# The first mixer's work and loads put into two written-out orders, and the sweep's raw weight tiles given places of their own

## The chip, the core and the metric

The kernel runs on one core of a Trainium2 chip. The metric is the device time of one execution in microseconds (us). Three executions of the kernel before took 917.3, 917.93 and 917.94 us; the median is 917.93 us. A change of about 0.2% (1.8 us) is what a measurement of this kernel can tell from none.

## The reference, cut to what matters

A decoder of two layers on 512 tokens of width 1024, float32. Layer 0 mixes tokens by pooling, layer 1 by a gated spatial unit; each is followed by a squared-ReLU MLP of width 4096. Six vectors per layer (shift, scale and gain for the mixer and for the MLP) come from one conditioning vector `c`.

```
mod = silu(c) @ ada_w[i] + ada_b[i];  sh1, sc1, g1, sh2, sc2, g2 = split(mod, 6)
h = rmsnorm(x, norm_mix_g[i]) * (1 + sc1) + sh1
layer 0:  y = per group of 256 channels: (windowed mean over 2, 4, 8, 16 tokens - h) @ pool_w, * pool_scale
x = x + g1 * y
h = rmsnorm(x, norm_mlp_g[i]) * (1 + sc2) + sh2
x = x + g2 * (square(relu(h @ w1[i])) @ w2[i])
```

The change touches the first mixer and the start of the first MLP only.

## The kernel before, in words

The big products run in three passes of high and low parts (`mm3`, L123: lines 125, 126, 127 of the profile are those passes), so TensorE (PE) is what most of the span is made of. VectorE (DVE) and ScalarE (ACT) prepare operands; every large load is issued by SyncE (SP) through one queue, in the order in which SP's instructions stand.

**The mixer** works on four groups of 256 channels, `g` = 0 to 3. What it needs from memory, in tiles of 512 KB:

- `x`, four tiles; `m`, 16 columns of `ada_w` (four a group, name `m` + group + number), each multiplied with silu(c) and summed by one DVE instruction (`column`, L251 to L255);
- the gains: for groups 0 and 1 two tiles `ag` that PE multiplies (`gains`, L285), for groups 2 and 3 two columns `gt` each (`gain_cols`, L295) that PE spreads over the partitions (`gain_spread`, L305);
- `pw`, the pooling weights, 256 KB a group, scaled by the gain in `weigh` (L309).

Per group: `windows` (PE, L324) takes the windowed means of x, `fin` (DVE, L269 to L274) finishes scale and shift from the four columns, `pooled` (ACT, L330) applies them, `product` (PE, L338) multiplies with pw, `add` (DVE, L345) adds into x, `sums_of` (L214 on ACT, L216 on DVE) sums squares for the next norm, `turn` and `turned` (PE L357, ACT L361) transpose x into `xf`. When the sums of all four groups are there, POOL takes the root (`power`, L168), ACT and DVE build diagonals, and PE spreads the norms (`rb`, L470).

**The sweep** (L475 to L489) is the first part of the MLP's first product: for each of eight blocks `k` of 128 channels, seven banks each get three matmuls, 168 in all. Block k needs `ht` (DVE L478), `hh` (ACT L479), `hl` (DVE L482), the weight tile `raw` of 448 KB (`sweep_load`, L380) split into a high part (ACT L386) and a low part (DVE L389), and, for the block's scale and shift, two more columns of `ada_w` (`ada`, L368).

Places in SBUF: the pool `w4` has three tiles, the pools `wh` and `wl` five each. Columns and gain tiles of the mixer take these 13 places in turn (`get_any`, L246); the sweep's `raw` tiles take `w4` places too (L381), and its columns go on taking all 13 in turn. A load into a place waits until the tile's last reader is done.

The order of DVE's and ACT's instructions in the mixer and the sweep is that in which the code is written (L391 to L487, from `gains(0)` on: group by group, in the order 0, 1, 2, 3); PE's is too. SP's order is left to the scheduler, which starts from the order in which the loads are written beside their consumers.

Of the kernel before, what the change touches and what calls it, by code (L numbers as in the profile page):

```python
# [35 lines left out]
def c_sc(n, k):  # L36
    return 24 * n + 2 * k
# [6 lines left out]
def c_g(n, k):  # L44
    return 24 * n + 16 + k


@with_exitstack
def decoder_kernel(ctx: ExitStack, tc: tile.TileContext, xtok, vecs, rows, fgrow, ada0, adag, ada1, pool_w, w1s, w1, w2, w2e, w_v, w_u, w_o, wsT, lnp, bs, out):
# [46 lines left out]
    shift(sm, 88)  # L96
# [81 lines left out]
    with (  # L178
        tc.tile_pool(name="st", bufs=1) as st,
        tc.tile_pool(name="st2", bufs=2) as st2,  # L180
        tc.manual_schedule(engines={mybir.EngineType.DVE, mybir.EngineType.Activation}),
# [40 lines left out]
        V.tensor_copy(cab, ca.unsqueeze(2).to_broadcast([P, KD, P]))  # L222
# [20 lines left out]
        slots = [(w4, "w4")] * 3 + [(wts, "wh"), (wts, "wl")] * 5
        nslot = [0]

        def get_any():  # L246
            pool, tag = slots[nslot[0] % len(slots)]
            nslot[0] += 1
            return pool.tile([P, D], F32, name="ada", tag=tag) if pool is w4 else wtile(tag, F32)

        def column(src, out):  # L251

            r = get_any()
            nc.sync.dma_start(r, src)
            V.scalar_tensor_tensor(r, r, 1.0, cb, ALU.mult, ALU.mult, accum_out=out)  # L255
# [3 lines left out]
        def m(g, *js):

            if g not in pm4:
                pm4[g] = sm.tile([P, 4], F32, name="pm4", tag="pm4")
            for j in js:
                column(ada0[4 * g + j], pm4[g][:, j : j + 1])

        def fin(g):
            win = 2 << g
            c, k = slice(4 * g, 4 * g + 4), slice(2 * g, 2 * g + 2)
            V.tensor_tensor(mods[0][:, c], pm4[g], vec[:, V_ADAB + c.start : V_ADAB + c.stop], ALU.add)  # L269
# [4 lines left out]
            V.tensor_tensor(bg, bg, sh, ALU.subtract)  # L274
# [3 lines left out]
        pw = st.tile([P, KD, 256], F32, name="pw")  # L278
        pgs, dgs = {}, {}

        def load_pw(g):
            c = slice(2 * g, 2 * g + 2)
            nc.sync.dma_start(pw[:, c], pool_w[:, c])

        def gains(g):  # L285
            po = pgs[g] = bank("pg", xz)[:, 0:256]
            for j in range(2):
                r = get_any().rearrange("p (k c) -> p k c", k=4)
                nc.sync.dma_start(r, adag[g, j])
                for k in range(4):  # L290
                    T.matmul(po, cab[:, 4 * j + k], r[:, k], start=(j + k == 0), stop=False)  # L291
            T.matmul(po, ones[0:1, :], row[0:1, D + 256 * g : D + 256 * g + 256], start=False, stop=True)
# [87 lines left out]
        def sweep_load(k):  # L380
            r = w4.tile([P, D], F32, name="raw", tag="w4")  # L381
            nc.sync.dma_start(r[:, 0 : P * SWEEP], w1s[k])
# [8 lines left out]
        gains(0)  # L391
        windows(0)
        m(0, 0, 1)
        weigh(0)
        m(0, 2, 3)
        fin(0)
        pooled(0)
        windows(1)
        gains(1)
        m(1, 0, 1)  # L400
        product(0)
        weigh(1)
        m(1, 2)
        add(0, 0)
        add(0, 1)
        m(1, 3)
        fin(1)
        pooled(1)
        for t in range(NT):
            sums_of(0, t)  # L410
        windows(2)
        gain_cols(2)
        product(1)
        turn(0)
        turned(0)
        gain_spread(2)
        m(2, 0)
        add(1, 0)
        weigh(2)
        m(2, 1)  # L420
        add(1, 1)
        m(2, 2, 3)
        fin(2)
        pooled(2)
        for t in range(NT):
            sums_of(1, t)
        windows(3)
        turn(1)
        turned(1)
        gain_cols(3)  # L430
        product(2)
        gain_spread(3)
        m(3, 0)
        weigh(3)
        m(3, 1)
        add(2, 0)
        add(2, 1)
        m(3, 2, 3)
        fin(3)
        pooled(3)  # L440
        for t in range(NT):
            sums_of(2, t)
        turn(2)
        turned(2)
        s3 = sm.tile([P, NT], F32, name="s3", tag="rv4")
        V.tensor_reduce(s3, ssg[:, :, 0:3], mybir.AxisListType.X, ALU.add)
        V.tensor_scalar(s3, s3, RMS_EPS, None, ALU.add)
        ada(0, 0)
        ada(0, 1)
        sweep_load(0)  # L450
        product(3)
        add(3, 0)
        sums_of(3, 0)
        sums_of(3, 1, V)
        sweep_hi(0)
        add(3, 1)
        sums_of(3, 2)
        sums_of(3, 3, V)
        V.tensor_tensor(s3, s3, ssg[:, :, 3], ALU.add)
        r4 = power(s3, NT)  # L460
        sweep_lo(0)
        turn(3)
        diag = st.tile([P, NT, P], F32, name="diag")
        rb = bank("rb", xz)
        for t in range(NT):
            if t % 2:
                V.tensor_scalar(diag[:, t], ident, r4[:, t : t + 1], None, ALU.mult)
            else:
                A.activation(diag[:, t], ident, AF.Copy, scale=r4[:, t : t + 1])
            T.matmul(rb[:, tok[t]], ones, diag[:, t], start=True, stop=True)  # L470
        turned(3)
        ada(1, 0)


        sweep = [bank("po") for _ in range(4)] + [bank("po", xz) for _ in range(SWEEP - 4)]  # L475
        for k in range(KD):
            t = st2.tile([P, S], F32, name="ht", tag="ht")
            V.scalar_tensor_tensor(t, xf[:, k], scl[0][1][:, k : k + 1], rb, ALU.mult, ALU.mult)  # L478
            A.activation(hh[:, k], t, AF.Identity, bias=mod(0, c_sh(1, k)))  # L479
            if k and k + 1 < KD:  # L480
                ada(k + 1, 0)
            V.scalar_tensor_tensor(hl[:, k], t, mod(0, c_sh(1, k)), f32(hh[:, k]), ALU.add, ALU.subtract)  # L482
# [481 lines left out]
```

## Time and profile before

| what | value |
|---|---|
| median of three executions | 917.93 us |
| the profiled execution's own time | 919.2 us |
| its span in the trace | 917.1 us |
| PE busy, share of the span | 877.8 us, 96% |
| DVE busy | 653.8 us, 71% |
| ACT busy | 419.9 us, 46% |
| POOL busy | 54.3 us, 6% |
| read from memory | 135.87 MB |
| mean granted clock of TensorE | 0.984 |

The times below are those of the profiled execution, counted from the start of its span, so they are compared with 917.1 and not with the median. The first sweep matmul starts at 74.99 us, the last of the 168 at 129.09 us. PE counts as busy while a matmul is in flight, at whatever clock, so a busy share near 100% can still hide slow matmuls: one of 512 columns takes a step of 0.23 us at the full granted clock and 0.43 us at half.

### The profile page before, as it was taken

What the parts mean: (1) busy time and instruction counts of PE and PEld (TensorE: products, weight loads), DVE (VectorE), ACT (ScalarE), POOL (GpSimd) and SP (SyncE); (2) the same over time, 40 slices, a digit from 0 to 9 for tenths busy, and PEclk for the clock granted to TensorE, in tenths of its full rate; (3) what the DMA queues carried; (4) which work ended last, traced back from release to release, by engine and by line L of the source; (5) the groups of instructions that cost most, each with busy time, mean ns of one, the idle gap of its engine ahead of it and who ended that gap; (6) DMA issues with size and microseconds to landing.
All of it is one profiled execution on the core that took longest, in us unless ns stands there. A gap on an engine that the chain in (4) does not pass through costs nothing.

```text
span 917.1 us, 10446 instructions
## 1 busy us (share of the span) xinstructions
PE 877.8 (96%) x3980; PEld 723.3 (79%) x3980; DVE 653.8 (71%) x846; ACT 419.9 (46%) x609; POOL 54.3 (6%) x102
## 2 busy tenths in 40 slices
PE   8766899999999999999999999999999999999996
PEld 5655678878888888888878888988887888888885
DVE  4855679778886888955798845557677576667954
ACT  4343375544544445436532425645545444444521
POOL 6000000300000000000310000000004000000000
PEclk9977999999999999999999999999999999999999
DMA  9915676355355342442547412741433134112212
GB/s 339 410 51 179 226 245 228 138 184 195 132 194 198 132 163 90 150 172 92 184 178 243 139 38 98 267 163 46 160 138 125 36 116 171 58 48 91 92 46 91
DMA packets 35475, 138.64 MB, mean 151 GB/s; under 512 B 3937, under 2 KB 4065, under 8 KB 32225
## 3 DMA queue, kind: packets, MB, share of 16 engines
q1 hardware_dynamic: 35282, 137.72, 42.2%
q8 instruction: 31, 0.51, 0.2%
q10 hardware_dynamic: 144, 0.26, 0.1%
q14 instruction: 18, 0.15, 0.0%
HBM read 135.87 MB, written 2.10 MB: 150 GB/s over the span
## 4 chain that ended last, share of the span: by engine, by line
PE 87%; DVE 5%; DMA 3%; ACT 2%; issue 1%; SPq 0%; POOL 0%; POOLq 0%; DVEq 0%; ACTq 0%
PE po L126 16%; PE po L127 16%; PE po L125 16%; PE pm L126 11%; PE pm L127 11%; PE pm L125 11%; DMA wh<-in_ada 2%; PE po L338 1%; PE pg L291 1%; DMA ada<-in_adag 1%; PE po L813 1%; DVE wl L255 1%; PE pb L161 1%; DVE wh L255 1%; DVE wl L389 1%
## 5 line engine op out<-in xcount | busy, mean ns | idle before, releaser
L125 PE MATMUL po<-hh,wl 128*128 128x512 f32 (+1 forms) x608 | 233.9, 385 | 7.7 <-ACT hh L479 7.7
L126 PE MATMUL po<-hl,wh 128*128 128x512 f32 (+1 forms) x608 | 232.6, 383 | 3.8 <-DVE hl L482 2.5
L127 PE MATMUL po<-hh,wh 128*128 128x512 f32 (+1 forms) x608 | 231.6, 381 | 0.0
L117 DVE TENSOR_TENSOR wl<-b,wh 128x1024 fp32r<-128x1024 f32 x84 | 102.7, 1224 | 70.1 <-ACT wh L116 70.0
L117 DVE TENSOR_TENSOR wl<-raw,wh 128x1024 fp32r<-128x1024 f32 x89 | 108.7, 1223 | 47.7 <-ACT wh L116 47.3
L125 PEld LDWEIGHTS po<-hh,wl 128*128 128x128 f32 x608 | 115.5, 190 | 32.0 <-ACT hh L479 9.7
L126 PEld LDWEIGHTS po<-hl,wh 128*128 128x128 f32 x608 | 115.5, 190 | 28.6 <-DVE hl L482 5.0
L127 PEld LDWEIGHTS po<-hh,wh 128*128 128x128 f32 x608 | 115.4, 190 | 21.3
L127 PE MATMUL pm<-wh,oh 128*128 128x512 f32 x336 | 130.7, 389 | 0.0
L125 PE MATMUL pm<-wh,ol 128*128 128x512 f32 x336 | 130.7, 389 | 0.0
L126 PE MATMUL pm<-wl,oh 128*128 128x512 f32 x336 | 130.7, 389 | 0.0
L116 ACT ACTIVATE wh<-raw 128x1024 fp32r<-128x1024 f32 x89 | 94.2, 1058 | 52.5 <-PE pm L127 33.4
L517 ACT ACTIVATE g<-po 128x512 f32<-128x512 f32 x64 | 37.9, 598 | 167.1 <-PE po L127 167.1
L116 ACT ACTIVATE wh<-b 128x1024 fp32r<-128x1024 f32 x84 | 88.4, 1053 | 14.2 <-PE pm L127 9.6
L147 DVE SCALAR_TENSOR_TENSOR ada<-ada,cb 128x1024 f32<-128x1024 f32 x56 | 68.2, 1221 | 16.6 <-DMA ada<-in_ada 16.5
L125 PEld LDWEIGHTS pm<-wh,ol 128*128 128x128 f32 x336 | 63.1, 188 | 13.2
L126 PEld LDWEIGHTS pm<-wl,oh 128*128 128x128 f32 x336 | 63.1, 188 | 13.1
L127 PEld LDWEIGHTS pm<-wh,oh 128*128 128x128 f32 x336 | 63.1, 188 | 13.0
L699 ACT ACTIVATE tmp<-x 128x512 f32<-128x512 f32 (+1 forms) x25 | 15.3, 613 | 64.9 <-DVE x L695 64.9
L617 DVE TENSOR_TENSOR y<-y,pm 128x512 f32<-128x512 f32 x68 | 43.4, 680 | 0.0
L518 ACT ACTIVATE g<-g 128x512 f32<-128x512 f32 x64 | 39.6, 624 | 0.0
L158 POOL TENSOR_SCALAR dg<-ident,mods 128x128 f32<-128x128 f32 x24 | 25.6, 1083 | 227.6 <-DVE wl L117 129.2
(164 smaller groups left out, 1163.1 us busy)
## 6 DMA issues: line engine op xcount, KB each, us to landing
ada<-in_ada SPq DMA_DIRECT2D x64, 512.0 KB, 3.3
raw<-in_w SPq DMA_DIRECT2D x57, 512.0 KB, 3.3
b<-in_w SPq DMA_DIRECT2D x24, 1024.0 KB, 4.8
raw<-in_w2e SPq DMA_DIRECT2D x16, 512.0 KB, 3.3
wh<-in_ada SPq DMA_DIRECT2D x14, 512.0 KB, 9.5
wl<-in_ada SPq DMA_DIRECT2D x14, 512.0 KB, 9.5
ur<-in_w_u SPq DMA_DIRECT2D x8, 512.0 KB, 5.9
raw<-in_w_v SPq DMA_DIRECT2D x8, 512.0 KB, 4.6
```

What stands on the lines that cost most here:

```text
L116: A.activation(h, r, AF.Copy)
L117: V.tensor_tensor(l, r, f32(h), ALU.subtract)
L125: T.matmul(o, wl, mh, start=first, stop=False, **kw)
L126: T.matmul(o, wh, ml, start=False, stop=False, **kw)
L127: T.matmul(o, wh, mh, start=False, stop=last, **kw)
L147: V.scalar_tensor_tensor(r, r, 1.0, cb, ALU.mult, ALU.mult, accum_out=pmv[i, b][:, j : j + 1])
L158: G.tensor_scalar(dg[:, k], ident, cols[:, k : k + 1], None, ALU.mult)
L255: V.scalar_tensor_tensor(r, r, 1.0, cb, ALU.mult, ALU.mult, accum_out=out)
L517: A.activation(t, po, AF.Relu)
L518: A.activation(t, t, AF.Square)
L617: V.tensor_tensor(yt, yt, banks[hf], ALU.add)
L699: A.activation(tmp, xt, AF.Square, scale=D**-0.5, accum_out=s[:, len(cs) : len(cs) + 1])
```

## The change

1. The mixer and what follows it up to the sweep is no longer written as calls in a row. A string `WORK` lists each piece of work (`m03`: the column 3 of group 0; `win`, `pd`, `pr`, `ad`, `sm`, `tn`, `td`: windows, pooled, product, add, sums, turn, turned; `gm`, `gt`, `gc`, `bc`, `we`: gain product, gain column, its finish, its spread, weigh; `hi`, `lo`: the split of a raw tile), and a loop carries them out in that order. A string `LOADS` lists the loads in their own order; a load is emitted as soon as the reader that its place waits for has been emitted. The four groups are now interleaved, and groups 0, 2, 1, 3 reach their product in that order.
2. SP joins the engines whose order is kept as written.
3. The sweep's `raw` tiles have two places of their own (pool `st2`). The sweep's columns (`n`) take only the three `w4` places.
4. The partial columns of each group have their own small tiles; `fin` forms the window term in one DVE instruction instead of two. Padding of the small pool goes from 88 to 64 words, and the large tiles that stay keep their addresses.

After the sweep the order of the instructions differs only within the first few units of the MLP.

```diff
+LOADS = """
+    gt20 m01 m03 gt31 x m02 m00 ag0 m22 gt21 m33 m20 pw0 m23 m21 m13 pw2 m12 ag1 m10 pw1 m11 pw3 m31 m32
+    gt30 m30 n01 raw0 n00
+"""
+WORK = """
...
+    gt30 pd1 pr2 m30 ad20 pr1 hi0 ad10 gc3 tn0 m31 win3 td0 ad11 fin3 ad21 pd3 bc3 sm11 sm03 sm12 we3
+    tn1 sm10 lo0 pr3 ad30 sm21 sm20 sm23 sm22 sm00 sm13 s3 sm30 sm31V ad31 td1 tn3 sm32 sm33V tot tn2
...
+"""
-        tc.manual_schedule(engines={mybir.EngineType.DVE, mybir.EngineType.Activation}),
+        tc.manual_schedule(engines={mybir.EngineType.DVE, mybir.EngineType.Activation, mybir.EngineType.SP}),
...
+        def places(name):
+
+            kind = name.rstrip("0123456789")
+            if kind == "n":
+                return slots[0:1]
+            return [slots[(nslot[0] + j) % len(slots)] for j in range({"ag": 2, "m": 1, "gt": 1}.get(kind, 0))]
...
+            def free(pool, tag):
+                bufs = 3 if pool is w4 else 5
+                return len(taken[tag]) < bufs or taken[tag][-bufs]
+
+            while queue and all(free(*at) for at in places(queue[0])):
+                load(queue.pop(0))
...
-            V.tensor_scalar(bg, sh, float(win), 1.0 / win, ALU.mult, ALU.mult)
-            V.tensor_tensor(bg, bg, sh, ALU.subtract)
+            V.scalar_tensor_tensor(b0[:, k], sh, win * (1.0 / win), sh, ALU.mult, ALU.subtract)
...
         def sweep_load(k):
-            r = w4.tile([P, D], F32, name="raw", tag="w4")
+            r = st2.tile([P, D], F32, name="raw", tag="raw")
             nc.sync.dma_start(r[:, 0 : P * SWEEP], w1s[k])
-            wk[k] = r[:, 0 : P * SWEEP], *(t[:, 0 : P * SWEEP] for t in wpair())
+            wk[k] = [r[:, 0 : P * SWEEP]]
 
         def sweep_hi(k):
+            wk[k] += [t[:, 0 : P * SWEEP] for t in wpair()]
             A.activation(wk[k][1], wk[k][0], AF.Copy)
...
+        for op in WORK.split():
+            on_v, op = op.endswith("V"), op.rstrip("V")
...
+            loads()
...
         for k in range(KD):
-            A.activation(hh[:, k], t, AF.Identity, bias=mod(0, c_sh(1, k)))
-            if k and k + 1 < KD:
-                ada(k + 1, 0)
+            norm_hi(k)
             if k + 1 < KD:
-                sweep_load(k + 1)
+                queue += [f"n{k + 1}0", f"raw{k + 1}", f"n{k + 1}1"]
+                loads()
+                n_(k + 1, 0)
+                norm_lo(k)
                 sweep_hi(k + 1)
-                ada(k + 1, 1)
+                n_(k + 1, 1)
                 sweep_lo(k + 1)
```

On SP, from the mixer's last loads into the sweep, the order before was this (`raw` are the sweep's weight tiles; `ada`, `wh` and `wl` with source `in_ada0` are columns, named by the place that they take):

```order
L254 DMA wh_487<-in_ada0 128x1024
L254 DMA wl_490<-in_ada0 128x1024
L382 DMA raw_496<-in_w1s 128x896
L254 DMA ada_544<-in_ada0 128x1024
L382 DMA raw_558<-in_w1s 128x896
L254 DMA ada_563<-in_ada0 128x1024
L254 DMA ada_595<-in_ada0 128x1024
L382 DMA raw_599<-in_w1s 128x896
L382 DMA raw_640<-in_w1s 128x896
L382 DMA raw_681<-in_w1s 128x896
L254 DMA wh_604<-in_ada0 128x1024
L254 DMA wl_636<-in_ada0 128x1024
```

Now it is this, from the last columns of the mixer (`wh_284`: gt30, `wl_287`: m30) on:

```order
L280 DMA wh_284<-in_ada0 128x1024
L280 DMA wl_287<-in_ada0 128x1024
L280 DMA ada_326<-in_ada0 128x1024
L430 DMA raw_328<-in_w1s 128x896
L280 DMA ada_330<-in_ada0 128x1024
L280 DMA ada_551<-in_ada0 128x1024
L430 DMA raw_553<-in_w1s 128x896
L280 DMA ada_555<-in_ada0 128x1024
L280 DMA ada_592<-in_ada0 128x1024
L430 DMA raw_594<-in_w1s 128x896
L280 DMA ada_596<-in_ada0 128x1024
```

Each block now loads one column, its raw tile and its other column, in the order in which they are used; before, three raw tiles stood ahead of a block's second column.

On DVE, up to the end of `fin(3)`, the place before (`wh_442` to `wl_456` are the columns m30 to m33; `po` are products of group 2; `mods0`, `scl00`, `b0` are fin's):

```order
L255 SCALAR_TENSOR_TENSOR wh_442,pm4_441<-wh_442,cb_89 128x1024
L312 TENSOR_TENSOR gp_445<-pg_439,psb_175 128x256
L314 TENSOR_TENSOR pw_202<-pw_202,gp_445 128x512
L255 SCALAR_TENSOR_TENSOR wl_448,pm4_441<-wl_448,cb_89 128x1024
L345 TENSOR_TENSOR x_96<-x_96,po_429 128x2x256
L345 TENSOR_TENSOR x_96<-x_96,po_434 128x2x256
L255 SCALAR_TENSOR_TENSOR wh_453,pm4_441<-wh_453,cb_89 128x1024
L255 SCALAR_TENSOR_TENSOR wl_456,pm4_441<-wl_456,cb_89 128x1024
L269 TENSOR_TENSOR mods0_90<-pm4_441,vec_78 128x4
L270 SCALAR_TENSOR_TENSOR scl00_92<-mods0_90,vec_78 128x2
L273 TENSOR_SCALAR b0_201<-mods0_90 128x2
L274 TENSOR_TENSOR b0_201<-b0_201,mods0_90 128x2
```

and now (`wl_281`: m32, `wh_284`: gt30, `wl_287`: m30, `wh_271`: m31; `po_391` is group 2, `po_403` and `po_408` are the halves of group 1):

```order
L311 SCALAR_TENSOR_TENSOR wl_281,pm4_177<-wl_281,cb_89 128x1024
L311 SCALAR_TENSOR_TENSOR wh_284,pmg_181<-wh_284,cb_89 128x1024
L311 SCALAR_TENSOR_TENSOR wl_287,pm4_177<-wl_287,cb_89 128x1024
L392 TENSOR_TENSOR x_96<-x_96,po_391 128x2x256
L392 TENSOR_TENSOR x_96<-x_96,po_403 128x2x256
L348 TENSOR_TENSOR pmg_181<-pmg_181,vec_78 128x2
L311 SCALAR_TENSOR_TENSOR wh_271,pm4_177<-wh_271,cb_89 128x1024
L392 TENSOR_TENSOR x_96<-x_96,po_408 128x2x256
L324 TENSOR_TENSOR mods0_90<-pm4_177,vec_78 128x4
L325 SCALAR_TENSOR_TENSOR scl00_92<-mods0_90,vec_78 128x2
L328 SCALAR_TENSOR_TENSOR b0_173<-mods0_90 128x2
```

`weigh` of group 3 has moved from between the columns to behind `fin(3)`, and the second add of group 1 now stands ahead of `fin(3)`.

On ACT, from `pooled(3)` to the diagonals of the norm, the order before (`sq`: sums of squares; `xf`: turned; `diag`: diagonals):

```order
L330 ACTIVATE pd_463<-pq_395,b0_201,scl00_92 128x512
L330 ACTIVATE pd_465<-pq_400,b0_201,scl00_92 128x512
L214 ACTIVATE sq_170,ssg_204<-x_96 128x256 x4
L361 ACTIVATE xf_203<-px_471 128x512
L361 ACTIVATE xf_203<-px_476 128x512
L376 ACTIVATE mods0_90<-pm2_486,vec_78 128x1 x2
L378 ACTIVATE scl01_93<-mods0_90,vec_78 128x1
L214 ACTIVATE sq_170,ssg_204<-x_96 128x256
L386 ACTIVATE wh_498<-raw_496 128x896
L214 ACTIVATE sq_170,ssg_204<-x_96 128x256
L469 ACTIVATE diag_531<-ident_84,rr_518 128x128 x2
```

and now:

```order
L377 ACTIVATE pd_449<-pq_432,b0_173,scl00_92 128x512
L377 ACTIVATE pd_451<-pq_437,b0_173,scl00_92 128x512
L233 ACTIVATE sq_166,ssg_183<-x_96 128x256 x11
L408 ACTIVATE xf_182<-px_461 128x512
L408 ACTIVATE xf_182<-px_466 128x512
L233 ACTIVATE sq_166,ssg_183<-x_96 128x256
L459 ACTIVATE diag_185<-ident_84,rr_510 128x128 x2
```

Eleven sums of squares now stand between `pooled(3)` and the last transposes, where four stood; the split of the first raw tile has moved ahead of `pooled(3)`.

More of the change, by code (lines that the diff above doesn't have):

```diff
@@ L45, in c_g @@
     return 24 * n + 16 + k
+LOADS = """
[3 more added lines that the diff above has]
+WORK = """
+    rowc rowp cab m03 gt20 sq0 m01 sq3 sq1 sq2 gt31 rms m02 gm0 m00 fin0 bandr m22 gt21 m33 gc2 we0 m23
+    m20 win0 m13 win2 bc2 pd0 m21 pr0 win1 m12 ad01 fin2 pd2 we2 ad00 m10 m11 sm02 fin1 gm1 sm01 we1 m32
+    gt30 pd1 pr2 m30 ad20 pr1 hi0 ad10 gc3 tn0 m31 win3 td0 ad11 fin3 ad21 pd3 bc3 sm11 sm03 sm12 we3
+    tn1 sm10 lo0 pr3 ad30 sm21 sm20 sm23 sm22 sm00 sm13 s3 sm30 sm31V ad31 td1 tn3 sm32 sm33V tot tn2
+    n01 diag td3 n00 td2
+"""
 @with_exitstack
@@ L93, in decoder_kernel @@
     gb = big.tile([P, D], F32, name="gb")
[L96 removed]
+    shift(sm, 64)
     def mod(i, c):
@@ L259, in m, with rms, bands @@
[L259 to L264, printed above, removed]
+        bandr = st.tile([P, NT, 4, W], F32, name="bandr")
+        rt = []
+        def rms():
+            v0 = sm.tile([P, NT], F32, name="rv4", tag="rv4")
+            V.tensor_scalar(v0, ss, RMS_EPS, None, ALU.add)
+            rt.append(power(v0, NT))
+        def bands():
+            for t in range(NT):
+                A.activation(bandr[:, t], band[:, 1 if t else 0], AF.Copy, scale=rt[0][:, t : t + 1])
@@ new lines, in loads, with take, column @@
+        def loads():
+            def free(pool, tag):
[3 more added lines that the diff above has]
+                load(queue.pop(0))
+        def take(name, j=0):
+            r, tag, n = tiles.pop((name, j))
+            taken[tag][n] = True
+            return r
+        def column(name, out):
+            r = take(name)
+            V.scalar_tensor_tensor(r, r, 1.0, cb, ALU.mult, ALU.mult, accum_out=out)
@@ L266, in fin, with m @@
+        b0 = st.tile([P, KD], F32, name="b0")
+        pm4 = [sm.tile([P, 4], F32, name="pm4", tag=f"pm4{g}", bufs=1) for g in range(4)]
+        pmg = [sm.tile([P, 2], F32, name="pmg", tag=f"pmg{g}", bufs=1) for g in range(4)]
+        def m(g, j):
+            column(f"m{g}{j}", pm4[g][:, j : j + 1])
         def fin(g):
@@ L389, in sweep_lo @@
             V.tensor_tensor(wk[k][2], wk[k][0], f32(wk[k][1]), ALU.subtract)
[L391 to L456, printed above, removed]
@@ L471, in decoder_kernel, with sum3, tot, spread_norms @@
-        turned(3)
-        ada(1, 0)
+        s3 = sm.tile([P, NT], F32, name="s3", tag="s3", bufs=1)
+        diag = st.tile([P, NT, P], F32, name="diag")
+        ht, rbs = {}, []
+        def sum3():
+            V.tensor_reduce(s3, ssg[:, :, 0:3], mybir.AxisListType.X, ALU.add)
+            V.tensor_scalar(s3, s3, RMS_EPS, None, ALU.add)
+        def tot():
+            V.tensor_tensor(s3, s3, ssg[:, :, 3], ALU.add)
+            rt.append(power(s3, NT))
+        def spread_norms():
+            rbs.append(bank("rb", xz))
+            for t in range(NT):
+                r = rt[1][:, t : t + 1]
+                if t % 2:
+                    V.tensor_scalar(diag[:, t], ident, r, None, ALU.mult)
+                else:
+                    A.activation(diag[:, t], ident, AF.Copy, scale=r)
+                T.matmul(rbs[0][:, tok[t]], ones, diag[:, t], start=True, stop=True)
@@ new lines, in norm_hi, with norm_lo @@
+        def norm_hi(k):
+            t = ht[k] = st2.tile([P, S], F32, name="ht", tag="ht")
+            V.scalar_tensor_tensor(t, xf[:, k], scl[0][1][:, k : k + 1], rbs[0], ALU.mult, ALU.mult)
+            A.activation(hh[:, k], t, AF.Identity, bias=mod(0, c_sh(1, k)))
+        def norm_lo(k):
+            V.scalar_tensor_tensor(hl[:, k], ht.pop(k), mod(0, c_sh(1, k)), f32(hh[:, k]), ALU.add, ALU.subtract)
+        work = dict(
+            rowc=lambda: spread_row(cb, 0, AF.Silu),
+            rowp=lambda: spread_row(psb, D + S, AF.Copy),
+            cab=lambda: V.tensor_copy(cab, ca.unsqueeze(2).to_broadcast([P, KD, P])),
+            sq=lambda t: squares(ss[:, t : t + 1], t, slice(0, D), (V, A)[t % 2]),
+            sm=sums_of, rms=rms, bandr=bands, m=m, n=n_, fin=fin, gm=gm, gt=gt, gc=gc, bc=bc, we=we,
+            win=windows, pd=pooled, pr=product, ad=add, tn=turn, td=turned, s=lambda _: sum3(), tot=tot,
+            diag=spread_norms, hi=sweep_hi, lo=sweep_lo,
+        )
@@ L475, in decoder_kernel @@
+        loads()
+        for op in WORK.split():
+            on_v, op = op.endswith("V"), op.rstrip("V")
+            kind, d = op.rstrip("0123456789"), [int(c) for c in op if c.isdigit()]
+            if on_v:
+                sums_of(*d, V)
+            else:
+                work[kind](*d)
+            loads()
         sweep = [bank("po") for _ in range(4)] + [bank("po", xz) for _ in range(SWEEP - 4)]
         for k in range(KD):
-            t = st2.tile([P, S], F32, name="ht", tag="ht")
-            V.scalar_tensor_tensor(t, xf[:, k], scl[0][1][:, k : k + 1], rb, ALU.mult, ALU.mult)
```

101 lines of the change are left out of this document (42 added, 59 removed).

## The prediction

> **What bounds the kernel now.** I read the page's first lines, then the busy time by stretches, because a mean over the span hides where PE waits.
>
> ```profile
> span 917.1 us, 10446 instructions
> ...
> 16.30:30.00 13.70, 13.70 (x77) 11.49 (x76) 10.65 (x22) 2.65 (x4) 0.00 (x0) 1.00 1.03 413
> ...
> 50.00:60.00 10.00, 4.10 (x20) 2.92 (x18) 6.31 (x14) 0.67 (x1) 0.00 (x0) 0.84 0.00 0
> ...
> 75.00:129.10 54.10, 45.55 (x168) 34.13 (x169) 34.78 (x50) 21.96 (x45) 0.00 (x0) 0.91 0.59 207
> 129.10:180.00 50.90, 50.90 (x226) 42.17 (x225) 41.93 (x45) 32.46 (x46) 7.17 (x8) 1.00 0.58 208
> ```
>
> Columns are PE, its weight load, DVE, ACT and POOL busy, then granted clock, DMA share and GB/s. Behind the sweep PE is busy all of the time at the full clock, so what comes later is a block of fixed length that starts when the sweep ends: a microsecond won ahead of 129.1 us is one won at the end. Ahead of it stand two stages. The mixer first runs at 413 GB/s, the transfers' pace, and then has 10 us with none at all (0 GB/s in 50 to 60). The sweep takes 54 us.
>
> The queue of SP and who held it up come next: the loads' issues, then SP's waits in the first 130 us, then the engines' waits within the sweep.
>
> ```profile
> 16.11 0.33 SPq L254 DMA_DIRECT2D wl<-in_ada  x1
> 17.39 0.33 SPq L254 DMA_DIRECT2D wh<-in_ada  x1
> ...
> 40.74 0.33 SPq L382 DMA_DIRECT2D raw<-in_w1s  x1
> 69.97 2.81 SPq L254 DMA_DIRECT2D ada<-in_ada  x2
> ```
>
> ```profile
> SPq L254 <- DVE wl L389: 27.8, 2, 21.7
> ```
>
> ```profile
> DVE wh L255 <- DMA wh<-in_ada: 15.8, 5, 6.2
> ...
> PE po L125 <- ACT hh L479: 7.7, 5, 2.3
> PE po L126 <- DVE hl L482: 2.5, 5, 0.6
> ```
>
> A column of 512 KB passes every 1.28 us (16.11 to 17.39). Between 40.74 and 69.97 SP issues nothing: its next column wants a w4 place that a raw tile of the sweep holds until DVE has split it (L389, 21.7 us of waiting at once). So the sweep's loads start when the sweep starts; there DVE waits 15.8 us for columns, and PE passes 10.2 us of that on.
>
> **The mixer, step by step.** Durations, in the order DVE, PE, ACT:
>
> ```profile
> 14.83 1.22 DVE L255 SCALAR_TENSOR_TENSOR ada<-ada,cb 128x1024 f32<-128x1024 f32 x1 [3.12 <-DMA ada<-in_ada]
> ...
> 41.23 1.22 DVE L255 SCALAR_TENSOR_TENSOR wh<-wh,cb 128x1024 f32<-128x1024 f32 x1
> ...
> 42.37 1.22 DVE L255 SCALAR_TENSOR_TENSOR wl<-wl,cb 128x1024 f32<-128x1024 f32 x1
> ...
> 55.06 1.28 DVE L345 TENSOR_TENSOR x<-x,po 128x512 f32<-128x512 f32 x2
> ...
> 58.66 0.16 DVE L269 TENSOR_TENSOR mods<-pm,vec 128x4 f32<-128x4 f32 x1
> ...
> 59.13 0.16 DVE L274 TENSOR_TENSOR b<-b,mods 128x2 f32<-128x2 f32 x1
> ...
> 68.26 0.42 DVE L216 SCALAR_TENSOR_TENSOR sq<-x 128x256 f32<-128x256 f32 x1 [0.58 <-ACT sq L214]
> ```
>
> ```profile
> 10.70 6.57 PE L291 MATMUL pg<-ada,cab 128*128 128x256 f32 x16 [0.23 <-DMA ada<-in_adag]
> ...
> 23.49 1.89 PE L291 MATMUL pg<-wh,cab 128*128 128x256 f32 x8
> 25.31 0.69 PE L292 MATMUL pg<-row,ones 1*128 1x256 f32 x2
> ...
> 29.49 2.08 PE L324 MATMUL pq<-bandr,x 128*128 128x144 f32 x16
> 33.11 3.96 PE L338 MATMUL po<-pw,pd 128*128 128x256 f32 x16 [1.55 <-ACT pd L330]
> 36.91 1.04 PE L357 MATMUL px<-ident,x 128*128 128x128 f32 x8
> ...
> 60.16 5.75 PE L338 MATMUL po<-pw,pd 128*128 128x256 f32 x16 [2.89 <-ACT pd L330]
> ...
> 74.99 0.80 PE L125 MATMUL po<-hh,wl 128*128 128x512 f32 x1 [1.66 <-ACT hh L479]
> ```
>
> ```profile
> 33.62 0.41 ACT L214 ACTIVATE sq<-x 128x256 f32<-128x256 f32 x1
> ...
> 34.16 0.42 ACT L214 ACTIVATE sq<-x 128x256 f32<-128x256 f32 x1
> ...
> 59.33 1.45 ACT L330 ACTIVATE pd<-pq,b,scl 128x512 f32<-128x512 f32 x2 [10.02 <-DVE b L274]
> ```
>
> *Transfers.* Before, m00 was behind four tiles of x, two of ag and a half-size pw, so it was unit 7.5 of 512 KB, and it landed at 14.8. Unit n then lands at 14.8 + 1.28 x (n - 7.5). In the new order the second half of ag0 is unit 12 (20.6 us) and m30, the last column that the mixer needs, unit 30 (43.6 us). No place holds this up: each reused place was read well ahead (the place of n01 is that of m21, read about 33; its load is issued some 8 transfers ahead of its landing, about 35). The total is as before; the order alone moves.
>
> *PE.* It stands idle from the row products until ag0 lands. I take the gain product at the slow row (6.57 for 16): from 19.3, when the first half lands, to 25.9, plus 0.6. Then it has work in a row: three windows 6.2 (2.08 each), the spread 0.5, three products 11.4 (3.8 each, 33.11 to 36.91), ag1's product 4.4 (1.89 twice and 0.6). That is 22.5, so group 1's product ends at 49.0. The route over DVE (m30 at 43.6, one column behind as m32, gt30 and group 1's weigh stand ahead: 1.15; m30 and m31 at 1.14 each; three adds at 0.6; fin 0.6) reaches 49.5, so both routes meet. `fin(3)` waits for the add of that product: 49.0 + 0.7 + 0.6 = 50.3, where it ended at 59.3 before. This is the main gain of the mixer: 9 us.
>
> *The tail.* The transpose of group 0 (1.0) and windows 3 (2.1) follow on PE: 52.1; the second half of `pooled(3)` ends at 53.0. The third product's cover is gone here: weigh(3), now behind fin(3), and group 1's transpose let product 3 start at 53.6, to 57.4 at the faster row. It doesn't set the end: ACT has ten sums of squares at 0.54 (33.62 to 34.16), 53.0 + 5.4 = 58.4, then one of group 3 (58.95), DVE's sum and add (60.2), ACT's next sum (60.85), and DVE's last sum starts at 60.9. From that instruction (68.26 before) to the first sweep matmul (74.99) the chain over POOL, diagonals, rb, ht and hh is the same, 6.73; I get **67.6**, which is 7.4 earlier. The tail behind fin(3) is longer (17.3 against 15.7), so 1.6 of the 9 is given back to ACT. The instruction saved in each fin is under 0.2 and is in the 0.6.
>
> Both ends: if PE stays at the slow row's pace for products 2, 1 and 3 (5.75 - 3.96, 1.8 each) and pro rata for ag1's product, windows 3 and the transpose (7.5 x 0.45 = 3.4), 8.8 comes on top and the start is about 76. If PE's first product is fast and DVE no column behind (1.2), and ACT's sums fit between other work, so that product 3's end at 57.4 decides (2.0), the start is 64.4.
>
> **The sweep, step by step.**
>
> ```profile
> 81.07 0.55 PE L126 MATMUL po<-hl,wh 128*128 128x512 f32 x1
> ...
> 82.37 0.39 PE L125 MATMUL po<-hh,wl 128*128 128x512 f32 x1
> ...
> 87.59 0.39 PE L127 MATMUL po<-hh,wh 128*128 128x512 f32 x1
> ```
>
> ```profile
> 74.97 0.75 DVE L482 SCALAR_TENSOR_TENSOR hl<-ht,mods,hh 128x512 fp32r<-128x512 f32 x1 [0.85 <-ACT hh L479]
> ...
> 79.59 0.75 DVE L482 SCALAR_TENSOR_TENSOR hl<-ht,mods,hh 128x512 fp32r<-128x512 f32 x1
> ```
>
> ```profile
> 80.08 6.47 DMA wh<-in_ada
> ...
> 89.27 4.18 DMA wh<-in_ada
> ```
>
> 23 steps from 82.37 to 87.59 make 0.227 us a matmul, 168 of them 38.1 us, 4.77 a block. The first 13 steps (74.99 to 81.07) took 6.1 instead of 3.0, and with the next one 3.3 us were lost to the lower clock and the first hl. I take the same loss, as PE's tail is as broken up as before: 41.4. The Trainium skill, "TensorE: Matmul & The Clock Gate", Part 1 (the HAM clock gate), says that a free-running window of about 3.4 us decides, and that one busy window brings the full clock; by it the half-speed stretch is 3.4 to 6.8 us, the loss 1.7 to 3.4 and the stage 39.8 to 41.5. The trace's 6.1 us lies inside.
>
> DVE's turn where it waits for no load is 4.6 a block (74.97 to 79.59), below PE's 4.77, so PE sets the pace if the loads keep up. Block 1's first column and raw tile now land at about 49; the block's second column waits for a place until n01 is read at about 62. Later a column's place comes free five to seven DVE instructions (5.3 us or more) ahead of its use, and a landing took 4.2 when little else was in flight (89.27). 2.9 units a block at 1.28 are 3.7 us of transfer, below 4.77. What is late next is the end: DVE splits two tiles of the next unit ahead of the last hl, where one split stood, at most 1.2; I take 0.5. The sweep takes **41.9** instead of 54.3 and ends at 109.5 instead of 129.3. Its 12.4 and the mixer's 7.4 make 19.8.
>
> The profiled execution took 2.1 more than its span and 1.3 more than the median of 917.93; the sum gives 897.3 of span, and 917.93 - 19.8 = **898.1** for the median.
>
> A page speaks against the mixer's share: the Trainium skill, "DMA: Bandwidth & Descriptors", Bandwidth, gives about 358 GB/s as the most that memory delivers to a core. That would make a unit 1.46, m30 land 4 us later, and the sum about 902. The trace's 413 GB/s in 16.3 to 30 stands against it.
>
> **The rivals.**
>
> *Three w4 places are too few.* With landings of 6.5 us (80.08, five loads in flight) against 5.3 of cover, each of blocks 2 to 7 waits 1.3: 7.8, so 905.9. For it: raw and two columns are issued close together. Against: never more than three wait for one block.
>
> *The mixer's gain is lost,* by products at the slow row (8.8 above): 906.9. For it: product 3 ran slow before. Against: PE now has work in a row from 26 to 52.
>
> *Slower transfers,* as at 324 GB/s for all of the mixer (10.5 to 16.3 had that):
>
> ```profile
> 10.50:16.30 5.80, 5.60 (x13) 4.54 (x14) 1.91 (x4) 3.23 (x7) 4.19 (x12) 1.00 0.95 324
> ```
>
> 1.62 a unit, m30 at 51, start about 75: 905.7. One dip of 6 us is not 30.
>
> *Slower than before:* each block leaves PE idle long enough that the clock stays at half. 168 at the pace of the first 13 steps (6.1 / 13 = 0.47) make 79 us, 24.5 more than now, less 7.4 from the mixer: 935. It decides from a sweep of 62 us. For it: the first block began so. Against: a block is 9 us of unbroken work at that pace, and before, 6 us of it sufficed for the full clock.
>
> *No change:* the lost start (8.8), landings of 6.5 (7.8) and one more dip in the transfers (5.8 us at 324 for 413: 1.3) come together: 916 and up. That the order isn't as written is closed by the lists.
>
> **How the numbers follow.** Forecast 0.67 (its own range 893 to 904), three places 0.11, lost mixer 0.09, slower transfers 0.03, no change 0.04, slower 0.06. The likeliest gives 898. Low end: a start at 64.4 (3.2) and a sweep of 39.8 (2.1) give 892.8, rounded down to 892; the high end takes in the three cases near 906: 907. Faster by over 0.2% (1.8 us, about what a measurement can tell): 0.90; same 0.04; slower 0.06.
>
> **What would show it.** Right: fin(3) ends near 50; the sweep's first matmul starts at 64 to 70; SP has no pause of 20 us ahead of the sweep's second block; PE's waits in the sweep fall from 10.2 to under 3; the stretch behind the sweep stays 100% busy. Wrong: fin(3) at 55 or later (mixer), DVE waiting over 5 us for `ada` within the sweep (places), granted clock under 0.9 over the sweep (clock).

## The result, and the profile after

Four executions of the kernel after took 895.78 to 897.34 us, median **896.27**; four of the kernel before 917.3 to 919.54, median 917.93. The ratio is 0.976, with a 95% interval of 0.975 to 0.978. The profiled execution took 895.87 us, 1.7 more than its span.

First the page's first line and the busy time by stretches; the columns are those shown of before.

```profile
span 894.2 us, 10448 instructions
...
16.30:30.00 13.70, 11.46 (x56) 9.77 (x57) 12.05 (x25) 5.52 (x10) 1.94 (x1) 1.00 1.02 400
50.00:60.00 10.00, 6.76 (x33) 6.09 (x32) 5.12 (x13) 7.20 (x27) 1.61 (x1) 0.84 0.00 1
64.40:105.80 41.40, 41.18 (x169) 33.49 (x170) 36.93 (x55) 22.92 (x46) 0.00 (x0) 0.93 0.88 297
105.80:180.00 74.20, 74.20 (x325) 60.78 (x324) 58.21 (x63) 42.93 (x58) 6.48 (x8) 1.00 0.55 192
```

The sweep is 41.4 us of nearly unbroken PE work (41.18 busy) with transfers at 297 GB/s beside it, where it took 54.1 at 207. Behind it PE is still busy all of the time. The row of 50 to 60 shows that there are still 10 us without transfers ahead of the sweep; the kernel simply reaches that point earlier.

PE's row, from the first gain product to the sweep:

```profile
18.54 3.75 PE L339 MATMUL pg<-wl,cab 128*128 128x256 f32 x8 [8.18 <-DMA wl<-in_adag]
22.09 2.19 PE L339 MATMUL pg<-wh,cab 128*128 128x256 f32 x8
...
38.73 7.17 PE L385 MATMUL po<-pw,pd 128*128 128x256 f32 x32
45.74 1.04 PE L404 MATMUL px<-ident,x 128*128 128x128 f32 x8
46.62 2.08 PE L371 MATMUL pq<-bandr,x 128*128 128x144 f32 x16
...
50.47 3.69 PE L385 MATMUL po<-pw,pd 128*128 128x256 f32 x16 [0.46 <-DVE pw L361]
...
57.16 3.22 PE L404 MATMUL px<-ident,x 128*128 128x128 f32 x14 [2.78 <-DVE x L392]
60.81 1.16 PE L460 MATMUL rb<-diag,ones 128*128 128x128 f32 x8 [0.43 <-ACT diag L459]
64.40 0.79 PE L147 MATMUL po<-hh,wl 128*128 128x512 f32 x1 [2.43 <-ACT hh L465]
```

Group 1's product ends at 45.74 and windows 3 just ahead of 48.6. The sweep's first matmul starts at **64.40** (74.99 before). The last of the 168 is followed by the next unit's first matmul at 105.77 (129.31 before), so the stage takes 41.37 us, where it took 54.32. The start is 10.6 earlier, the sweep 12.95 shorter: 23.5 at its end, of which the span keeps 22.9. Of the 0.6 given back, 0.5 is one later wait for a low part `hl` behind the sweep (1.7 us for 1.2).

DVE's row to the end of fin(3), and its last sum of squares:

```profile
41.45 1.22 DVE L311 SCALAR_TENSOR_TENSOR wl<-wl,cb 128x1024 f32<-128x1024 f32 x1 [0.48 <-DMA wl<-in_ada]
...
44.01 1.23 DVE L311 SCALAR_TENSOR_TENSOR wl<-wl,cb 128x1024 f32<-128x1024 f32 x1
45.16 1.28 DVE L392 TENSOR_TENSOR x<-x,po 128x512 f32<-128x512 f32 x2
46.43 1.22 DVE L311 SCALAR_TENSOR_TENSOR wh<-wh,cb 128x1024 f32<-128x1024 f32 x1
...
48.44 0.15 DVE L328 SCALAR_TENSOR_TENSOR b<-mods 128x2 f32<-128x2 f32 x1
...
55.53 0.17 DVE L445 TENSOR_REDUCE s<-ssg 128x4 f32<-128x12 f32 x1 [2.37 <-ACT sq L233]
57.68 0.42 DVE L235 SCALAR_TENSOR_TENSOR sq<-x 128x256 f32<-128x256 f32 x1 [0.58 <-ACT sq L233]
```

From the landing of m32 (41.45) to fin(3) (ends at 48.59; 59.3 before) DVE has no gap: it takes each column up as it lands, m30 at 44.01, and this route sets fin(3). Windows 3 on PE are ready in the same 0.1 us. Before, DVE stood still at `weigh(3)`, which waited for PE's spread of the gain, with three of the four columns of group 3 behind it:

```profile
52.85 0.42 DVE L312 TENSOR_TENSOR gp<-pg,psb 128x256 f32<-128x256 f32 x1 [4.96 <-PE pg L307]
```

So of the 10.7 us that fin(3) ends earlier, 2.7 are m30, taken up at 44.01 instead of 46.67, and 8.0 are what DVE no longer does or waits for between m30 and fin(3) (4.6 us instead of 12.6). Behind fin(3) DVE waits for ACT's sums (2.37 and 0.58). ACT's row there:

```profile
46.40 0.95 ACT L435 ACTIVATE wh<-raw 128x896 fp32r<-128x896 f32 x1 [4.94 <-DMA raw<-in_w1s]
...
47.84 1.06 ACT L408 ACTIVATE xf<-px 128x512 f32<-128x512 f32 x2
48.80 1.44 ACT L377 ACTIVATE pd<-pq,b,scl 128x512 f32<-128x512 f32 x2
50.12 0.42 ACT L233 ACTIVATE sq<-x 128x256 f32<-128x256 f32 x1
...
55.53 0.42 ACT L233 ACTIVATE sq<-x 128x256 f32<-128x256 f32 x1
```

ACT itself, busy with the split of the first raw tile since that landed and with the turned group 0, comes free for `pooled(3)` only at 48.80, so an earlier fin(3) alone would have won next to nothing. Then come ten sums in a row, one each 0.54 us from 50.12 on, and the eleventh at 55.53. Last, SP's issues, and what it waited for in 30 to 130 us:

```profile
36.46 0.33 SPq L280 DMA_DIRECT2D ada<-in_ada  x1
36.94 0.33 SPq L430 DMA_DIRECT2D raw<-in_w1s  x1
38.26 1.00 SPq L280 DMA_DIRECT2D ada<-in_ada  x2
40.16 0.33 SPq L430 DMA_DIRECT2D raw<-in_w1s  x1
59.48 2.86 SPq L280 DMA_DIRECT2D ada<-in_ada  x2
```

```profile
SPq L280 <- DVE ada L311: 35.2, 14, 18.0
```

SP still pauses for 19 us (40.5 to 59.48), now for n01's place. But both columns and the raw tile of block 0, and a column and the raw tile of block 1, were issued ahead of it.

### The profile page after: what moved, and what is told of

Its sections match the earlier page's. It is cut to its first block, busy times and chain, and to the rows that moved or that the text cites. A ratio compares the mean times of both kernels' runs of the same rounds, so it can differ in the third digit from the quotient of the medians.

```text
span 894.2 us, 10448 instructions
## 1 busy us (share of the span) xinstructions
PE 866.9 (97%) x3980; PEld 719.1 (80%) x3980; DVE 652.0 (73%) x842; ACT 419.8 (47%) x609; POOL 56.2 (6%) x102
## 4 chain that ended last, share of the span: by engine, by line
PE 89%; DMA 5%; DVE 3%; ACT 2%; issue 0%; POOL 0%; SPq 0%; POOLq 0%; DVEq 0%; ACTq 0%
PE po L148 18%; PE po L149 18%; PE po L147 17%; PE pm L148 11%; PE pm L149 11%; PE pm L147 11%; DMA ada<-in_ada 1%; DMA wh<-in_adag 1%; DMA wl<-in_ada 1%; PE po L828 1%; DMA wh<-in_ada 1%; PE pb L183 1%; DVE ada L311 1%; DVE x L392 0%; ACT wh L138 0%
```

## The experiments

Three groups of runs, each with its own runs of the kernel before; ratios are to those. Start and length are read from PE's rows as above. In the table, "queue" means that SP's order is that of `LOADS` and of the sweep's queue, kept as written.

| kernel | mixer's order | `raw` places | SP's order | sweep starts | takes | median | ratio (95%) |
|---|---|---|---|---|---|---|---|
| before | old | w4 | scheduler's | 74.99 | 54.32 | 918.63 | 1 |
| e1 | old | own | scheduler's | 75.95 | 54.13 | 917.8 | 0.999 (0.997 to 1.001) |
| e2 | new | w4 | queue | 64.34 | 51.22 | 905.6 | 0.986 (0.984 to 0.988) |
| e3 | old, in the new code | own | queue | 73.30 | 41.49 | 905.28 | 0.985 (0.984 to 0.987) |
| e4 | new | own | scheduler's | 64.49 | 40.49 | 895.36 | 0.975 (0.974 to 0.977) |
| e8 | old | own | as written | 73.62 | 41.26 | 907.43 | 0.989 (0.987 to 0.992) |

The median of before is that of the runs beside e1 to e4; beside e8 it was 918.23. Starts and lengths are each read from one execution, e1's from its slowest (923.24 us). The kernel after has a second trace, in e9: start 65.20, length 41.49; so differences of a start or a length under about 1 us say nothing here.

**e1: places of their own alone,** in the kernel before:

```
-            r = w4.tile([P, D], F32, name="raw", tag="w4")
+            r = st2.tile([P, D], F32, name="raw", tag="raw")
```

> The kernel before, with the sweep's raw tiles in two places of their own (pool st2); all orders are left as they were, SP's to the scheduler. Theory (two separate gains: the order of the mixer 10.6 us, unblocked loads of the sweep 13): SP has no 20 us pause any more, the sweep starts at 75 as before and takes 43 to 47 instead of 54; 906 to 911 us. Rival (places are worth nothing unless SP's order is kept too): the sweep stays above 50, 914 us or more. Second rival (the whole gain is the places): 896 to 899.

917.8: no difference, and the theory missed: SP's pause ahead of the sweep is still there (until 70.93), and the sweep takes 54.13. SP's issues in the sweep, and DVE's row there, say why:

```profile
87.30 0.33 SPq L382 DMA_DIRECT2D raw<-in_w1s  x1
87.67 0.43 SPq L254 DMA_DIRECT2D wh<-in_ada  x1
88.16 0.42 SPq L254 DMA_DIRECT2D wl<-in_ada  x1
```

```profile
86.18 1.09 DVE L389 TENSOR_TENSOR wl<-raw,wh 128x896 fp32r<-128x896 f32 x1
...
93.79 1.23 DVE L255 SCALAR_TENSOR_TENSOR wh<-wh,cb 128x1024 f32<-128x1024 f32 x1 [4.06 <-DMA wh<-in_ada]
```

The scheduler puts a raw tile two blocks ahead in front of the next block's columns. That raw tile waits for a place until the split at 86.18 ends (87.2), and the two columns, whose places are free, are issued right behind it, at 87.67 and 88.16; DVE waits 4.06 us for the first.

**e2: the new kernel with raw back in w4** (`raw` and the columns share the three places).

```
-            if kind == "n":
+            if kind in ("n", "raw"):
...
-            r = st2.tile([P, D], F32, name="raw", tag="raw")
+            r = w4.tile([P, D], F32, name="raw", tag="w4")
...
```

> The changed kernel, with the sweep's raw tiles back in the w4 places that its columns take; both written-out orders and SP's kept order stay. Theory: the sweep still starts at 64 to 66, but a block's second column then stands behind a raw tile that waits until the last one is split, so each block waits about 2 us: the sweep takes 52 to 58 instead of 41.4, 907 to 913 us. Rival (the order of the loads alone made the sweep fast): 41 to 43, 896 to 899 us.

905.6, with the sweep at 51.22, both a little below the theory's ranges. What the engines waited for shows the price of shared places with the new order:

```profile
DVE ada L311 <- DMA ada<-in_ada: 12.1, 7, 2.4
```

DVE waits 12.1 us for columns in the sweep; the kernel after does not.

**e3: the new code with both strings in the old order.**

```
 LOADS = """
+    x ag0 pw0 m00 m01 m02 m03 ag1 pw1 m10 m11 m12 m13 gt20 gt21 pw2 m20 m21 m22 m23 gt30 gt31 pw3
+    m30 m31 m32 m33 n00 n01 raw0
...
 WORK = """
+    cab rowc sq0 sq1 sq2 sq3 rms rowp bandr gm0 win0 m00 m01 we0 m02 m03 fin0 pd0 win1 gm1 m10 m11
...
+    sm33V tot lo0 tn3 diag td3
```

> The changed kernel with both tables written so that the mixer's work and loads stand in the order of before (groups 0, 1, 2, 3 one after the other); own places for raw, and SP's order kept. Theory: the sweep starts at 74 to 76 as before, and takes 41 to 43 as in the changed kernel: 905 to 908 us. Rival (the sweep is fast only because the new mixer order hands it over with DVE ahead): the sweep takes 47 or more, 912 us or more.

905.28 and a sweep of 41.49 are within the theory's ranges, the start of 73.30 is 0.7 below. The written order of the mixer is worth 8.9 us at the sweep's start, and nothing within the sweep.

**e4: the new kernel with SP's order left to the scheduler.**

```
-        tc.manual_schedule(engines={mybir.EngineType.DVE, mybir.EngineType.Activation, mybir.EngineType.SP}),
+        tc.manual_schedule(engines={mybir.EngineType.DVE, mybir.EngineType.Activation}),
```

> The changed kernel with SP's order left to the scheduler again; it then puts the raw tiles of blocks 2 and 3 next to each other, ahead of the columns of both (the one difference on any engine). Theory: the mixer is the same (sweep from 64.4); a block's columns stand behind a raw tile whose place is freed later, a wait of 1 to 4 us in all: 897 to 900 us. Rival (SP's kept order is what decides the sweep): sweep above 50, 905 us or more.

895.36: the expected loss did not come. Starting from the queue's order, the scheduler moves only a pair of raw tiles ahead of columns. So what counts is the order that results, not that SP keeps it. (895.36 and the 896.27 of the kernel after can't be told apart.)

**e8: the kernel before with own places and SP's order kept as written** (column, raw, other column for each block; the columns stay in all 13 places).

```
-            r = w4.tile([P, D], F32, name="raw", tag="w4")
+            r = st2.tile([P, D], F32, name="raw", tag="raw")
...
-        tc.manual_schedule(engines={mybir.EngineType.DVE, mybir.EngineType.Activation}),
+        tc.manual_schedule(engines={mybir.EngineType.DVE, mybir.EngineType.Activation, mybir.EngineType.SP}),
```

> The kernel before with two of the change's parts: raw tiles in places of their own, and SP's loads kept in the order in which the code is written (one column, raw, other column for each block); the mixer's order and the columns' 13 places stay as before. Theory (places and the order of the loads together make the sweep's gain, neither alone): the sweep starts at 74 to 76 us as before and takes 41 to 44 instead of 54.3, time 904 to 908. Rival (columns confined to the three w4 places, or the written-out queue, is needed too): the sweep takes 50 us or more, 914 or more.

907.43, start 73.62, sweep 41.26. SP's issues during the second block:

```profile
81.72 0.33 SPq L254 DMA_DIRECT2D wh<-in_ada  x1
82.10 0.43 SPq L254 DMA_DIRECT2D wl<-in_ada  x1
82.63 0.37 SPq L382 DMA_DIRECT2D raw<-in_w1s  x1
```

The columns now stand ahead of the raw tile. The two places settle the sweep together with this order (e8 41.26); the places alone do nothing (e1 54.13), and with the order but shared places it stays long (e2 51.22). In e2 raw tiles and columns share three places; the order alone, in the kernel before with its 13 places for the columns, was not run. Confining the columns to w4 is not needed. The start is 1.4 earlier than in before and 0.4 below the theory's range. The loads do not bring this: SP issues them in the same order as before until 40.7 us, and 1.0 of it is there by 30 us, where PE's first gain product began at 10.44 and took 5.84 us (10.70 and 6.57 before).

**e5: fewer sums on ACT behind pooled(3),** in the kernel after. `sm00` and `sm03` move to ACT's idle time near 37 us, `sm23` and `sm22` to DVE. DVE's sums also write their squares, which nobody reads, into `cab`, which is free by then; in the kernel after they go into the tile `sq` that ACT's sums write too.

```
-    ... sm02 fin1 gm1 sm01 we1 m32
+    ... sm02 fin1 gm1 sm01 sm00 sm03 we1 m32
...
-    tn1 sm10 lo0 pr3 ad30 sm21 sm20 sm23 sm22 sm00 sm13 s3 sm30 sm31V ad31 td1 tn3 sm32 sm33V tot tn2
+    tn1 sm10 lo0 pr3 sm23V sm22V ad30 sm13 sm21 sm20 sm30 sm31V s3 td1 ad31 tn3 sm32 sm33V tot tn2
...
+            if on is V and c.stop - c.start < D:
+                j = cab[:, 0:2].rearrange("p a b -> p (a b)")
```

> The kernel after, with ACT's sums of squares moved: two of group 0 into ACT's idle time near 37 to 40 us, and two of group 2 onto DVE, so that five instead of nine are left on ACT between pooled(3) and DVE's last sum. Theory (behind fin(3) the start of the sweep is set by ACT's sums, 0.54 us each): DVE's last sum starts at about 55 instead of 57.7, the sweep starts at 61.6 to 62.6 instead of 64.4, time 893.5 to 894.5. Rival (product 3, which ends at 54.0, or the work on POOL sets it): start within 0.7 us of 64.4, time 895.5 to 897.

894.49 (893.14 to 894.99). Seven sums instead of eleven now stand on ACT between `pooled(3)` and the last transposes. DVE's last sum, and PE's rows:

```profile
54.72 0.42 DVE L237 SCALAR_TENSOR_TENSOR cab<-x 128x256 f32<-128x256 f32 x1
```

```profile
54.74 1.75 PE L406 MATMUL px<-ident,x 128*128 128x128 f32 x14 [0.56 <-DVE x L394]
57.99 1.16 PE L462 MATMUL rb<-diag,ones 128*128 128x128 f32 x8 [1.49 <-ACT diag L461]
61.57 0.80 PE L147 MATMUL po<-hh,wl 128*128 128x512 f32 x1 [2.43 <-ACT hh L467]
```

The last sum starts at 54.72 for 57.68, the sweep at 61.57 for 64.40: in the kernel after ACT's sums did set the start, and product 3 (ended at 54.0) did not. In e5 DVE waits for no sum of ACT ahead of its own last one, but 0.29 us for product 3, which comes next. Part of the gain is the tile `cab`: in the kernel after DVE's last two sums each waited for a sum of ACT (0.17 and 0.58), in e5 they start without waiting. By these two waits it is 0.75 of the 2.8 us at most, the moved sums the rest; the two were not run apart.

**e6 and e7: the half clock at the sweep's start.** In the kernel after the sweep's first 13 steps took 6.2 us (64.40 to 70.59), about as before (6.1). e6 adds eight matmuls into a bank that nobody reads, between `rb` and the sweep; e7 does so in e5.

```
+            fl = bank("fl", xz)
...
+            for t in range(8):
+                T.matmul(fl[:, tok[t % NT]], ones, diag[:, t % NT], start=True, stop=True)
```

> The kernel after, with eight matmuls of 128x128 added on PE between the spread of the norms and the sweep's first matmul, into a bank that nobody reads, where PE stood idle for 2.4 us. Theory (the half clock from 63.5 to 70.3 us comes from that idle time): the sweep runs at the full clock from its start, its first 13 steps take 3 to 4 us instead of 6, the sweep takes 38.5 to 39.5 instead of 41.4 us, time 893.5 to 895. Rival (the idle time ahead is not what lowers the clock): the first 13 steps stay at about 6 us, time 896 to 898, the added matmuls costing up to 2 us.

> Both of the last two edits in one kernel. Theory: both gains add, start near 62, sweep near 39, time 891 to 892.5. Rival (they share the same idle time: with the sums gone PE has no gap, or the half clock comes back elsewhere): no better than the better one of the two, 893.5 or more.

e6 took 894.24 us, its sweep 39.55 (0.05 over the range), the first 13 steps 3.1 (65.20 to 68.27). Its ratio to before, 0.974 (0.972 to 0.976), is not clear of the 0.976 (0.975 to 0.978) of the kernel after. e7 took 892.2 (891.91 to 893.25): start 62.37, sweep 40.11. Busy time by stretches, first of after, then of e6, e5 and e7:

```profile
60.10:63.40 3.30, 1.44 (x10) 0.97 (x8) 2.22 (x5) 3.04 (x9) 0.22 (x1) 0.98 0.68 186
63.50:70.20 6.70, 5.58 (x12) 4.08 (x13) 6.70 (x12) 4.19 (x9) 0.00 (x0) 0.51 0.93 322
```

```profile
60.10:63.40 3.30, 2.94 (x13) 2.94 (x14) 2.27 (x6) 3.29 (x9) 0.00 (x0) 0.50 0.68 233
65.20:70.20 5.00, 5.00 (x25) 4.14 (x24) 5.00 (x9) 2.32 (x5) 0.00 (x0) 1.00 0.85 286
```

```profile
57.00:60.00 3.00, 1.16 (x8) 0.97 (x8) 1.64 (x5) 2.47 (x8) 0.50 (x1) 0.98 0.51 180
60.00:66.60 6.60, 4.81 (x11) 3.43 (x12) 6.60 (x11) 4.34 (x9) 0.00 (x0) 0.50 0.88 288
```

```profile
56.00:62.37 6.37, 4.24 (x37) 3.81 (x35) 4.53 (x9) 4.13 (x12) 1.93 (x1) 1.00 0.45 149
62.37:70.20 7.83, 7.31 (x31) 5.80 (x32) 7.83 (x14) 3.87 (x9) 0.00 (x0) 1.00 0.94 331
```

In e6 a half-clock stretch still comes. Read in slices of 0.1 us it lasts from 57.9 to 64.8: it begins 4.4 us ahead of the first added matmul (62.33), over the transposes, and is over when the sweep starts. So e6's numbers fit the theory, but the pause ahead of the sweep did not bring its half clock. The second trace of the kernel after (e9) has it from 58.8 to 69.0, begun ahead of that pause too. The pair e5 and e7 differs in the added matmuls alone, and there the low stretch (59.9 to 66.7 in e5) is gone: 1.00 throughout, and in e10, which is e7 again, as well. The mean granted clock of the whole execution was 0.997 or 0.998 in all nine executions of these two, and 0.993 to 0.996 in the four of e5. So with the sums moved the added work keeps the clock up; that the one pause of 2.4 us lowers it is not shown. What does is taken up in the last section.

e7's total is at the upper end of what the theory gave, because the sweep took 40.11 and not 39. Its first 13 steps took 3.9 us (62.37 to 66.28), as PE waits there for the first `hl`, and at the last block it waits once more. PE's rows of both, and DVE's row at the last block:

```profile
63.38 0.50 PE L148 MATMUL po<-hl,wh 128*128 128x512 f32 x1 [0.52 <-DVE hl L473]
...
97.81 0.50 PE L148 MATMUL po<-hl,wh 128*128 128x512 f32 x1 [0.76 <-DVE hl L473]
```

```profile
94.74 2.35 DVE L139 TENSOR_TENSOR wl<-raw,wh 128x1024 fp32r<-128x1024 f32 x2
97.01 0.75 DVE L473 SCALAR_TENSOR_TENSOR hl<-ht,mods,hh 128x512 fp32r<-128x512 f32 x1
```

The last hl stands behind two splits of the next unit (2.35 us), and PE, now faster, waits 0.76 for it. That it would go with another order was not tried.

**e9 and e10: after and e7 once more, side by side on one chip.**

> The kernel after, unchanged, beside the next kernel on one chip. Theory (the sums and the filler matmuls are worth 4 us): 895.5 to 897.5 us, with a ratio to the kernel before of 0.975 to 0.978. Rival (half of that difference was one of chips): 893.5 to 895.

> The kernel with both edits (sums moved, filler matmuls) a second time, beside the kernel after. Theory: 891.5 to 893.5 us, 3.5 to 4.5 below the kernel after, and no run of the one reaches into the runs of the other. Rival: less than 2 us below it.

897.09 (896.37 to 900.62) against 892.0 (891.12 to 892.62), with 0.977 and 0.970 (0.969 to 0.972) of before: 5.1 us, more than expected, and no run of one reaches into the other. e7 beats both kernels.

## Why the prediction came out

**The direction and the two parts** held: an earlier start and a shorter sweep, each shown by itself (e3 and e8 have the sweep's part, e2 the start's).

**The sweep** was put at 41.9: 38.1 of matmuls, 3.3 for the half clock and the first hl, 0.5 for a late end. It took 41.37. The first two terms are what the trace shows (the first block takes 8.05 us, those behind it 4.76 each: 72.45, 77.21, 81.97); the third came just behind the sweep, as 0.5 more of the wait for hl. The Trainium skill, "TensorE: Matmul & The Clock Gate", Part 1 (the HAM clock gate), had put the half-speed stretch at 3.4 to 6.8 us; in the trace the clock is at half from 63.6 to 70.5, 6.8 us, and 6.1 of them lie in the sweep. In e9, the same kernel, it is at half from 58.8 to 69.0, and 3.8 lie in the sweep.

**The start** was put at 67.6 and came at 64.40, right on the lower bound: this is the term that was mis-sized, by 3.2 (by 2.4 in e9's trace). That it met the bound to the tenth is luck: the bound was reached with ACT's sums hidden, so that product 3, ended at 57.4, decides; but the sums decided, and product 3 ended at 54.0. Of the 3.2, 1.7 lies ahead of the end of fin(3) (48.6 for 50.3). The step "PE has work in a row" had group 1's product at 49.0; it ended at 45.74, since the first gain product was at the slow pace for one half only (3.75, then 2.19; 6.57 had been taken for both), it began 0.8 sooner, and the work behind it took 20.9 for 22.5. So PE's route dropped out and DVE's decided: the sum for it had given 49.5, 0.9 too much: m30 landed at 43.98, 0.4 later than summed, but DVE took it up at once and was not a whole column behind. The other 1.5 lies in the tail (15.8 for 17.3), 1.2 of it because windows 3 were done in time, so that pooled(3) ended 1.5 after fin(3) and not 2.7. Which of the two routes comes last is close and changes with the execution: in e9 the first gain product began at 19.28 and took 3.75 and 2.79, group 1's product ended at 47.1 and windows 3 at 49.9, and the second half of `pooled(3)` waited for these, as the prediction had it, while fin(3) ended at 48.8. Why the first gain product is slow was left open: the granted clock reads 1.00 there. The step that ACT's sums, and not product 3, set the end of the tail is borne out by e5; the chain from DVE's last sum to the sweep (6.73) took 6.72.

**Transfers.** m30 was to land at 43.6 and landed at 43.98. The rate was 400 GB/s in 16.3 to 30, above the 358 of the Trainium skill ("DMA: Bandwidth & Descriptors", Bandwidth), so the sum by that figure (902) did not come. The same section of the Trainium skill gives about 358 as what each of two cores gets when both stream from one memory; here one core runs.

**The signs.** fin(3) near 50, the start at 64 to 70, PE's waits under 3 (2.4 and 0.2), the stretch behind the sweep at 100% and the clock over 0.9 (0.93) came as named. The 10.2 us of PE's waits before held 1.7 at the sweep's first matmul, which is the wait for its start, as the 2.4 is now; behind that they went from 8.5 to 0.2. The sign on SP was badly chosen: its pause of 19 us is still there, for a place again, but the loads of nearly two blocks were issued ahead of it, and DVE waits for no column of the sweep behind it.

**The rivals.** Three w4 places were not too few: DVE waits for no column in the sweep; with the raw tiles in them as well, as in e2, they are. Lost mixer gain and slower transfers did not occur. The half clock over the whole sweep did not come (0.93), and was not provoked in a run.

**What the prediction left open:** it gave the sweep's gain to earlier landings without saying which of own places and order of the loads was needed. Its reading of before, that a raw tile's place holds the queue up, is half of the cause: e1 was expected to show the places as enough, and showed them worth nothing without the order.

## What to carry to other kernels

In a queue that issues in order, a load that waits for its place holds up every load behind it: read in SP's rows what stands behind the waiting load before giving it another buffer, and change the order and the buffers together. Where an engine's row of small work stands between the last input and a barrier, as ACT's sums here, count it in that engine's order; moving four of eleven of them, with a scratch tile of DVE's own, was worth 2.8 us at the sweep's start. Thin work on PE ahead of a long run of matmuls can be paid twice, once as the pauses and once at half clock behind them; in e7 eight matmuls that nobody needs, put into a pause, kept the clock up.

## What was not expected of the hardware

The clock went down although PE had not been idle for a whole stretch: in the kernel after it was busy 1.44 of the 3.30 us from 60.1 to 63.4, at the full clock, and the next 6.7 us ran at half (0.51); with 4.24 busy of 6.37 in e7 it stayed full.

The traces show where the border lies, when the granted clock is read in slices of 0.1 us. In each of the ten traces in which it changes behind 38 us (before, after, e1 to e6, e8, e9) all changes lie on a grid of steps of 3.41 us. Before, for instance, it falls at 43.8, 57.5 and 71.1, which are four steps apart. In after it falls at 56.8 and 63.6 and rises at 60.2 and 70.5; in e9, the same kernel, it falls at 58.8 and rises at 69.0, so the grid lies elsewhere in another execution. Counted over these steps, from about 40 us to the end of the sweep:

| clock in the step | PE busy in the step | next step | how many |
|---|---|---|---|
| full | 0 to 1.72 us | half | 22 |
| full | 1.82 us or more | full | 136 |
| half | 2.98 us or less | half | 25 |
| half | 3.06 us or more | full | 22 |

So in these traces a step with about half of its time in PE work, or less, is followed by one at half clock, and only a step of nearly unbroken work brings the full clock back. In e5 the step ahead of the fall (56.5 to 59.9) held 1.18 us of work, with the pause ahead of `rb` and the beginning of the one ahead of the sweep in it. In e7 and e10, where the clock stayed full, no stretch of 3.41 us from 45 to 64 us holds less than 1.75. This was read from the traces afterwards; no run was made to test it.
